# First attention's scores as three products of split operands, its rows one slot later, rotary steps behind them, and a last scaling out of SBUF in 640 and 384 columns

## The chip, the core and the metric

One core of one Trainium2 chip runs the whole program in one launch. The metric is device time in microseconds (us), the median of several runs. The engines are PE (TensorE, with its weight loads listed apart as PEld), DVE (VectorE), ACT (ScalarE), POOL (GpSimd) and SP (SyncE, which here mostly issues DMAs). Each engine works through its own row of instructions in order and waits on semaphores for what the others produce.

## The reference

A decoder trunk of two layers on 256 tokens of 1024 channels. Each layer norms its input, projects it, runs three token mixers side by side (the first attention, MLA, with 8 heads of 64 + 32 query and key columns; MoBA; retention), gates and sums them, and adds an MLP of squared ReLU. A last norm ends it. What the change touches:

```
def mla_branch(cq, ckv, k_rope, q_norm_g, kv_norm_g, w_q_up, w_kv_up, cos, sin):
    q = (rms_norm(cq, q_norm_g) @ w_q_up)            # per head: 64 "nope" + 32 rotary columns
    q = concat([q[..., :64], apply_rope(q[..., 64:], cos, sin)])
    kv = (rms_norm(ckv, kv_norm_g) @ w_kv_up)        # per head: 64 key + 64 value columns
    k = concat([kv[..., :64], broadcast(apply_rope(k_rope, cos, sin))])
    o = causal_attention(q, k, kv[..., 64:], 96 ** -0.5)
...
return rms_norm(x, final_norm)                       # after the last layer
```

## The kernel before

**Split products.** Nearly all products run on operands split in two rounded parts: a value is copied by ACT to fp32r (`hi`), and DVE subtracts to get `lo`. A product is then the three products hi·hi, hi·lo and lo·hi, added in PSUM (`three`, L297 to L300). Weights are split the same way when they arrive from HBM: `raw` (DMA on SP), `whi` (ACT, L277), `wlo` (DVE, L279), with six buffers of each. A `whi` can be written when PE's last product on the buffer's former holder has ended.

**Stages.** The tokens are two row tiles of 128. The projections of a layer run one after another as units: the compressed columns and MoBA's mq and mk first, then mv, then the gates (gmla0, gmla1, gmoba0, gmoba1), retention's rqk, rv and rg, the last gate, the branches' outputs, the output projection and the MLP. A unit of projection has four slots (0 to 3), and a slot of a 512-column unit has 12 products of 512 columns, six for each row tile. In between mv's slots stand MLA's own three products: qrope (the query's rotary columns, in PSUM tile pqr), qnope (the query's other columns, two PSUM tiles nope), kvup (the keys, two more tiles nope, and the values pv). All have the turned compressed columns `cTh` and `cTl` as one operand.

**What sets the order.** The program is a list `prog` of units; other steps are hung on a slot by `at(slot(unit, j), step)`. `attention(...)` hangs its groups of four heads (scores, softmax, a bounce of the probabilities through HBM that turns them, values) on slots counted from `first`. A list scheduler then orders each engine's row from the dependences, so a step that is moved in the list also moves its neighbours on ACT and DVE.

**Buffers.** PSUM has eight banks: four of tag `acc` (`acc_tile`: the projections' accumulators, and qnope's two tiles) and four of tag `misc` (pqr, kvup's tiles, scores, values of attention). A new tile takes a bank when the last reader of its former holder is done. In SBUF the tag `t4` has eight buffers of 4 x 256 columns: the four parts of the layer's input `xs0` to `xs3`, `cTh`, `cTl`, and later the attentions' outputs in hi and lo (`omlah`, `omlal` and so on).

**MLA's operands before.** `Q` and `KK` are f32 tiles of 128 partitions x 8 heads x 256 tokens. The nope tiles are copied by ACT from PSUM (L949, L950: 64 partitions at a time). The rotary part of the query is copied from pqr to `qr`, a swapped copy `qkoth` is fetched by DMA, and `qr_rope` multiplies both by tables (L982) and adds them in four steps of 64 partitions on DVE, straight into `Q` (L985, L986). A score product (L1005) is one f32 matmul of 128 columns and one of 256 for each head.

**MoBA's steps.** `moba_rope` rotates the rows of mq and mk on DVE, turns them in blocks and writes them to HBM; `fetch_turned` reads them back turned (`mqT`, `mkT`, DMAs on SP); `order_queries` copies the queries into `qkT` on ACT. MoBA's scores are L551.

**The end.** The last norm (L1545 to L1567) squares each row tile's halves on ACT (`fsq`, with the row sums in `fst`), takes root (ACT) and reciprocal (DVE, `fr`), and scales: the first half was multiplied by the gain `gf` on DVE beforehand (L1560) and is scaled on ACT (L1566); the other goes from PSUM in one step on DVE (L1563). Each half has its own DMA to HBM, on SP and on ACT's queue.

Of the kernel before, what the change touches and what calls it, by code (L numbers as in the profile page):

```python
# [7 lines left out]
F32 = mybir.dt.float32  # L8
F32R = mybir.dt.float32r
BF16 = mybir.dt.bfloat16  # L10
AF = mybir.ActivationFunctionType
ALU = mybir.AluOpType
AX = mybir.AxisListType

P = 128
D = 1024
S = 256
# [16 lines left out]
MLA_H, MLA_QR, MLA_KVR, NOPE, ROPE, VD = 8, 256, 128, 64, 32, 64  # L34
QKD = NOPE + ROPE
# [9 lines left out]

C_QNOPE = [QKD * h + i for h in range(MLA_H) for i in range(NOPE)]
C_QROPE = [
    QKD * h + NOPE + 16 * half + i for p in range(0, MLA_H, 2) for half in range(2) for h in (p, p + 1) for i in range(16)
]

C_MQ, C_MK = range(416, 928), range(928, 1440)
# [98 lines left out]
def trunk(ctx: ExitStack, tc: tile.TileContext, gx, wts, consts, gfin, gn, xtok, out):  # L150


    nc = tc.nc
    _, where, _ = weight_plan()
# [3 lines left out]
    sb = ctx.enter_context(tc.tile_pool(name="sb", bufs=1))  # L158
# [10 lines left out]
    K = cp.tile([P, K_DEC], F32, name="K")  # L169
# [16 lines left out]
    def load_w(*key):  # L186

        ahead = 0 if key[:2] in ((0, "b0"), (0, "mq"), (0, "b0mq")) else AHEAD
        have(min(ahead + 1, len(loaded) + len(order)))
        return loaded.pop(key)  # L190
# [99 lines left out]

    def w2k(name):
        return sb.tile([P, 512], F32, name=name, tag="w2k", bufs=W2K)

    def t4(name):
        return sb.tile([P, 4, S], F32R, name=name, tag="t4", bufs=T4)

    def three(o, ah, al, bh, bl, start, stop, **more):  # L297
        nc.tensor.matmul(o, ah, bh, start=start, stop=False, **more)  # L298
        nc.tensor.matmul(o, ah, bl, start=False, stop=False, **more)  # L299
        nc.tensor.matmul(o, al, bh, start=False, stop=stop, **more)  # L300
# [4 lines left out]
    def halves(tile_):  # L305
        return tile_.rearrange("p (two s) -> p two s", two=2)
# [11 lines left out]
    def split_plain(src, hi, lo):  # L318
        return nc.scalar.activation(hi, src, AF.Copy), nc.vector.tensor_sub(lo, src, hi.bitcast(F32))  # L319
# [451 lines left out]
    def at(slot, step):  # L771
        steps.setdefault(slot, []).append(step)

    def slot(key, j):
        return [k for k, _ in prog].index((key, j))
# [9 lines left out]
    def layer(l, xn, before):  # L785

        c0 = []
        c, mla, mqkv, rqkv = {}, {}, {}, {}
# [101 lines left out]
        def moba_rope(key):  # L890
            rope_rows(mrows[key], K[:, K_ROT_MB:K_DEC], MB_D // 8, w2k("mrot"))
            bounces[key] = written_rows(mrows[key], key, blocks_tile(key))

        def fetch_turned(key):
            qkT[key] = read_turned(bounces[key], key + "T", "tsums" if key == "mq" else "exch")
# [21 lines left out]

        def c_turn():
            c["h"], c["l"] = t4("cTh"), t4("cTl")
            mla["Q"] = sb.tile([P, MLA_H, S], F32, name="Q", bufs=1)  # L920
            KK = mla["K"] = sb.tile([P, MLA_H, S], F32, name="KK", bufs=1)
            mla["v"] = [w2k("vml") for _ in range(NT)]
            pts = [misc_tile("pct") for _ in range(2)]
            for k in range(3):
                pt = pts[k // 2][:, (k % 2) * S : (k % 2) * S + S]
                for t in range(NT):
                    nc.tensor.transpose(pt[:, P * t : P * t + P], c0[t][0][:, P * k : P * k + P], ident)
            pkr = pts[1][:, S : 2 * S]
            for t in range(NT):
                nc.tensor.transpose(pkr[:, P * t : P * t + P], krx[t], ident)  # L930
            for k in range(3):
                pt = pts[k // 2][:, (k % 2) * S : (k % 2) * S + S]
                split(pt, c["h"][:, k, :], c["l"][:, k, :], gain(G_CQ + 3 * l + k))
            nc.scalar.copy(KK[0:64, 1::2, :], pkr[0:64, None, :].to_broadcast([64, 4, S]))
            nc.scalar.copy(KK[64:P, 0::2, :], pkr[64:P, None, :].to_broadcast([64, 4, S]))

        at(slot("mk", 1 if l else 2), c_turn)

        def nope(dst, w, ks, copy, bank):
            for b in range(2):  # L940
                acc = bank("nope")
                for i in range(2):
                    cs = slice(P * (2 * b + i), P * (2 * b + i) + P)
                    for j, k in enumerate(ks):
                        three(
                            acc[:, S * i : S * i + S], w[0][:, j, cs], w[1][:, j, cs], c["h"][:, k, :], c["l"][:, k, :],
                            j == 0, j == len(ks) - 1,
                        )
                copy(dst[0:64, 4 * b : 4 * b + 4 : 2, :], halves(acc)[0:64])  # L949
                copy(dst[64:P, 4 * b + 1 : 4 * b + 4 : 2, :], halves(acc)[64:P])  # L950

        def qrope():

# [11 lines left out]
            mla["qo"] = swapped(mla["qr"])  # L965

        def qnope():
            nope(mla["Q"], load_w(l, "qnope", 0), (0, 1), nc.scalar.copy, acc_tile)

        def kvup():  # L970
            wh, wl = load_w(l, "kvup", 0)
            nope(mla["K"], (wh[:, :, 0:512], wl[:, :, 0:512]), (2,), nc.scalar.copy, misc_tile)
            for t in range(NT):
                acc = misc_tile("pv")
                sl = slice(P * t, P * t + P)
                three(acc, c["h"][:, 2, sl], c["l"][:, 2, sl], wh[:, 0, 512:1024], wl[:, 0, 512:1024], True, True)
                nc.scalar.activation(mla["v"][t], acc, AF.Copy)

        def qr_rope():
            qr, qo = halves(mla["qr"]), halves(mla["qo"])  # L980
            for i, o in enumerate((qr, qo)):
                nc.vector.tensor_mul(o, o, TAB_MLA[:, S * i : S * i + S][:, None, :].to_broadcast([P, 2, S]))  # L982
            for b in range(2):
                rows = slice(64 * b, 64 * b + 64)
                nc.vector.tensor_add(mla["Q"][64:P, 2 * b :: 4, :], qr[rows], qo[rows])  # L985
                nc.vector.tensor_add(mla["Q"][0:64, 2 * b + 1 :: 4, :], qr[rows], qo[rows])  # L986

        project(l, "mv", xn, 512, moba_done("mv"))
        for i, unit in enumerate((qrope, qnope, kvup)):
# [3 lines left out]
        omlaT, omobaT, oretT = [], [], []  # L993
        th_mla = gates(l, "gmla", xn)
        for i, key in enumerate(("mq", "mk")):
            at(slot("mv", i), lambda key=key: moba_rope(key))
            at(slot("gmla0", 2 * i), lambda key=key: fetch_turned(key))
        first = slot("mv", 3)
        at(first, lambda: omlaT.extend((t4("omlah"), t4("omlal"))))

        def mla_scores(h0):
            banks = [misc_tile("ps_s") for _ in range(4)]
            for h, bank in enumerate(banks, h0):
                for o, qs, ks in ((slice(0, P), slice(0, P), slice(0, P)), (slice(P, 3 * P), slice(P, S), slice(0, S))):
                    nc.tensor.matmul(bank[:, o], mla["Q"][:, h, qs], mla["K"][:, h, ks], start=True, stop=True)  # L1005
            return banks

        mla_last = attention(
            omlaT, lambda: mla["v"], QKD, first, mla_scores, (), MLA_GAP, MLA_TURN, MLA_MOVED, ("probT", "KK"),
            (l, "rg", 1), range(0, 4) if l else range(4, 8),  # L1010
        )
# [16 lines left out]
        def order_queries(h0):  # L1028
            qkT["q", h0] = in_order(qkT["mq"], h0 // 2)

        for i in range(2):
            at(slot("gmla1", 1 + i), lambda i=i: order_queries(4 * i))
        first = slot("gmoba1", 1)
        at(first, lambda: omobaT.extend((t4("omobah"), t4("omobal"))))

# [429 lines left out]
        for kind, i in mlp_order(l)[: -ENDS[l]]:  # L1465
# [11 lines left out]
            else:  # L1477
                w = load_w(l, "down", i, 0)
                for q in quarters:
                    down(w, h2[i], *q, i)  # L1480
                if last and i == NF - 8:
                    gf = sb.tile([P, D], F32, name="gf", tag="t4", bufs=T4)
# [64 lines left out]
        for t in range(NT):  # L1547
            y = sb.tile([P, D], F32, name="y", tag="t4", bufs=T4)
            r = sb.tile([P, 1], F32, name="fr", tag="st", bufs=SMALL)
            s0, s1, s2 = (st[:, 3 * t + i : 3 * t + i + 1] for i in range(3))  # L1550
            for half in range(2):
                cs = slice(512 * half, 512 * half + 512)
                ends[2 * t + half]()
                acc = accs[2 * t + half]
                if t == 0:
                    x_add(t, half)
                square(acc, 3 * t + half)
                if half == 0:
                    nc.vector.tensor_scalar(s2, s0, EPS, None, op0=ALU.add)
                    nc.vector.tensor_mul(y[:, cs], acc, gf[:, cs])  # L1560
            nc.scalar.activation(s1, s1, AF.Sqrt, bias=s2)
            nc.vector.reciprocal(r, s1)
            nc.vector.scalar_tensor_tensor(y[:, cs], acc, r, gf[:, cs], op0=ALU.mult, op1=ALU.mult)  # L1563
            nc.sync.dma_start(out[:, t, cs], y[:, cs])
            cs = slice(0, 512)
            nc.scalar.activation(y[:, cs], y[:, cs], AF.Copy, scale=r)  # L1566
            nc.scalar.dma_start(out[:, t, cs], y[:, cs])  # L1567
        order_pe.close()
# [19 lines left out]
W2K = 17  # L1588
# [96 lines left out]
```

## Time and profile before

| | |
|---|---|
| median of 3 runs | 802.57 us (802.55 to 802.66) |
| profiled execution | 802.47 us, span 800.4 us, mean granted clock 0.998 |
| PE busy | 792.7 us, 99% of the span |
| DVE busy | 654.8 us, 82% |
| ACT busy | 493.4 us, 62% |
| HBM traffic | 242 GB/s over the span |

The span is the time from the first to the last instruction of the profiled execution. In the rows of the profile an instruction has its line, its operation, `out<-in` by the program's names, and its shape; in a timeline the first number is the start in us and the second the busy time in us (of one instruction or, with x16, of a stretch of sixteen). Matmuls are pipelined: the time that one takes from the next is the distance of their starts, not its own duration. In the list of waits a row reads: who waited, for whom, then the sum in us, how often, and the longest. A row of the chain is a step of the work that ended last.

### The profile page before, as it was taken

The numbers are of one execution on the slowest core, as the hardware profiler recorded it, in microseconds if no ns is written. First come the engines' busy times: TensorE is split into PE (matmuls) and PEld (weight loads), VectorE is DVE, ScalarE is ACT, GpSimd is POOL, SyncE is SP. The second block draws the span as 40 slices with busy tenths as digits, with TensorE's granted clock in tenths as the row PEclk, the third lists the DMA queues.
The fourth block names the chain that finished last, engine by engine and source line by source line (L and its number), as shares of the span: only waits on it lengthen the run. The fifth ranks groups of instructions, "written<-read, shape, count | busy, mean of one in ns | idle before, by whom it ended". The sixth has DMA issues, their size and how long they took to land.

```text
span 800.4 us, 11136 instructions
## 1 busy us (share of the span) xinstructions
PE 792.7 (99%) x3819; PEld 660.3 (82%) x3819; DVE 654.8 (82%) x1129; ACT 493.4 (62%) x750; POOL 29.0 (4%) x32
## 2 busy tenths in 40 slices
PE   9999999999999999999999999999999999999996
PEld 7888887888888888888888888888888888888885
DVE  6779678878888888887796986788698879999794
ACT  7786665544557666666477765654545666666562
POOL 0100000000030000000020000000001200000000
PEclk9999999999999999999999999999999999999999
DMA  9979967965667867777655889587665687688841
GB/s 340 371 243 288 314 207 222 320 216 151 249 218 242 276 221 230 266 266 236 234 165 194 275 290 305 185 281 245 230 234 174 193 271 278 225 299 298 265 162 53
DMA packets 70280, 194.74 MB, mean 243 GB/s; under 512 B 8016, under 2 KB 27856, under 8 KB 70224
## 3 DMA queue, kind: packets, MB, share of 16 engines
q1 hardware_dynamic: 69648, 193.17, 73.2%
q10 hardware_dynamic: 576, 0.87, 0.3%
q8 instruction: 30, 0.49, 0.2%
q14 instruction: 26, 0.21, 0.1%
HBM read 171.46 MB, written 22.02 MB: 242 GB/s over the span
## 4 chain that ended last, share of the span: by engine, by line
PE 99%; DVE 0%; issue 0%; ACT 0%
PE acc L298 19%; PE acc L300 19%; PE acc L299 19%; PE pup L299 8%; PE pup L298 8%; PE pup L300 8%; PE acc L1240 6%; PE acc L859 1%; PE ps_s L1005 1%; PE po L645 1%; PE ps_s L551 1%; PE warm L765 0%; PE po L647 0%; PE ps_r L551 0%; PE b L865 0%; PE b L868 0%
## 5 line engine op out<-in xcount | busy, mean ns | idle before, releaser
L277 ACT ACTIVATE whi<-raw 128x1024 fp32r<-128x1024 f32 (+3 forms) x263 | 265.1, 1019 | 169.9 <-PE acc L300 102.3
L279 DVE TENSOR_TENSOR wlo<-raw,whi 128x1024 fp32r<-128x1024 f32 (+3 forms) x263 | 305.2, 1176 | 70.3 <-ACT whi L277 67.7
L298 PE MATMUL acc<-whi,xs 128*128 128x512 f32 (+1 forms) x384 | 150.2, 393 | 0.0
L299 PE MATMUL acc<-wlo,xs 128*128 128x512 f32 (+1 forms) x384 | 149.6, 390 | 0.0
L300 PE MATMUL acc<-whi,xs 128*128 128x512 f32 (+1 forms) x384 | 149.2, 390 | 0.0
L299 PE MATMUL pup<-wlo,xs 128*128 128x512 f32 x256 | 100.0, 391 | 0.0
L300 PE MATMUL pup<-whi,xs 128*128 128x512 f32 x256 | 99.8, 390 | 0.0
L298 PE MATMUL pup<-whi,xs 128*128 128x512 f32 x256 | 99.5, 390 | 0.0
L298 PEld LDWEIGHTS acc<-whi,xs 128*128 128x128 f32 x384 | 72.2, 188 | 15.7 <-ACT whi L277 0.7
L300 PEld LDWEIGHTS acc<-whi,xs 128*128 128x128 f32 x384 | 72.2, 188 | 14.2
L299 PEld LDWEIGHTS acc<-wlo,xs 128*128 128x128 f32 x384 | 72.2, 188 | 13.9
L300 PE MATMUL acc<-whi,sq 128*128 128x512 f32 x184 | 71.9, 391 | 0.0
L298 PE MATMUL acc<-whi,sq 128*128 128x512 f32 x184 | 71.9, 391 | 0.0
L299 PE MATMUL acc<-wlo,sq 128*128 128x512 f32 x184 | 71.7, 390 | 0.0
L300 PEld LDWEIGHTS pup<-whi,xs 128*128 128x128 f32 x256 | 48.1, 188 | 9.8
L299 PEld LDWEIGHTS pup<-wlo,xs 128*128 128x128 f32 x256 | 48.1, 188 | 9.7
L298 PEld LDWEIGHTS pup<-whi,xs 128*128 128x128 f32 x256 | 48.0, 188 | 9.8
L300 PEld LDWEIGHTS acc<-whi,sq 128*128 128x128 f32 x184 | 34.5, 188 | 7.7 <-DVE sq L319 0.6
L299 PEld LDWEIGHTS acc<-wlo,sq 128*128 128x128 f32 x184 | 34.6, 188 | 7.1
L298 PEld LDWEIGHTS acc<-whi,sq 128*128 128x128 f32 x184 | 34.6, 188 | 7.0
L573 ACT ACTIVATE prob<-prob,smx 128x128 f32<-128x128 f32 x64 | 28.3, 443 | 18.5 <-DVE smx L570 18.5
L1240 PE MATMUL acc<-mT,whi 128*128 128x512 f32 (+1 forms) x144 | 35.2, 371 | 0.0
(277 smaller groups left out, 1205.1 us busy)
## 6 DMA issues: line engine op xcount, KB each, us to landing
raw<-wts SPq DMA_DIRECT2D x264, 512.0 KB, 4.8
bounce<-hblocks SPq DMA_DIRECT2D x16, 512.0 KB, 3.7
hturned<-bounce SPq DMA_DIRECT2D x64, 128.0 KB, 3.1
pbounce<-blocks SPq DMA_DIRECT2D x8, 768.0 KB, 5.7
probT<-pbounce SPq DMA_DIRECT2D x32, 192.0 KB, 5.5
raw<-wts SPq DMA_DIRECT2D x5, 464.0 KB, 6.4
raw<-wts SPq DMA_DIRECT2D x4, 416.0 KB, 4.3
dec<-consts SPq DMA_DIRECT2D x2, 768.0 KB, 8.2
```

What stands on the lines that cost most here:

```text
L277: fetched.append(nc.scalar.activation(hi[:, cs], raw[:, cs], AF.Copy))
L279: nc.vector.tensor_sub(lo[:, cs], raw[:, cs], hi[:, cs].bitcast(F32))
L298: nc.tensor.matmul(o, ah, bh, start=start, stop=False, **more)
L299: nc.tensor.matmul(o, ah, bl, start=False, stop=False, **more)
L300: nc.tensor.matmul(o, al, bh, start=False, stop=stop, **more)
L551: mm = nc.tensor.matmul(bank[:, o], a[rows, sa], b[rows, sb_], start=True, stop=True)
L573: nc.scalar.activation(p[:, a:b], p[:, a:b], AF.Exp, bias=m[:, 2 + i : 3 + i], scale=d**-0.5, accum_out=m[:, 4 + i : 5 + i])
L645: nc.tensor.matmul(dst, vh, pT[h + j][0], start=True, stop=False)
L859: nc.tensor.matmul(mq[t][:, cs], a[:, P * t : P * t + P], wq[part][:, cs], start=first, stop=stop)
L1005: nc.tensor.matmul(bank[:, o], mla["Q"][:, h, qs], mla["K"][:, h, ks], start=True, stop=True)
L1240: nc.tensor.matmul(o, a, b, start=half == 0 and i == 0, stop=4 * half + n == KD and i == len(jobs) - 1)
```

## The change

**Scores.** `Q` and `KK` become fp32r tiles that hold the hi parts; their lo parts are `Ql` and `KKl`, each two tiles (four heads apiece) out of tag `t4`. The nope copies become a split: a hi copy on ACT and a lo subtraction on DVE for each 64 partitions. The key's rotary part is split once into `kr` and copied by ACT to `KK` and `KKl`. The query's rotary part is summed whole in `qr` (one DVE step), copied whole to `qrh` (ACT), and from there to `Q` in four ACT copies and to `Ql` in four DVE subtractions. Each score product becomes `three` on 128 and on 256 columns. The order of heads in `C_QROPE` changes with it, so that four heads that share a tile lie together.

**Places.** MLA's first group comes at gmla0 slot 0, not mv slot 3. MoBA's rotary steps come at gmla0 slots 2 and 3, not mv 0 and 1; their fetches at gmla1 1 and 2, not gmla0 0 and 2; the ordered queries at gmoba0 0 and 1, not gmla1 1 and 2.

**End.** Both halves of the last norm are multiplied by `gf` on DVE ahead of the reciprocal; then DVE scales 640 columns out of SBUF and ACT 384, with a DMA each of those widths.

```
+        def w2r(name):
+            return sb.tile([P, 512], F32R, name=name, tag="w2k", bufs=W2K)
...
         def c_turn():
-            mla["Q"] = sb.tile([P, MLA_H, S], F32, name="Q", bufs=1)
-            KK = mla["K"] = sb.tile([P, MLA_H, S], F32, name="KK", bufs=1)
+            for key in ("Q", "KK"):
+                mla[key] = sb.tile([P, MLA_H, S], F32R, name=key, bufs=1), [t4(key + "l") for _ in range(2)]
+            (KK, KKl), kr = mla["KK"], w2r("kr")
...
-            nc.scalar.copy(KK[0:64, 1::2, :], pkr[0:64, None, :].to_broadcast([64, 4, S]))
-            nc.scalar.copy(KK[64:P, 0::2, :], pkr[64:P, None, :].to_broadcast([64, 4, S]))
+            split_plain(pkr, kr[:, :S], kr[:, S:])
+            for rows, odd in ((slice(0, 64), 1), (slice(64, P), 0)):
+                nc.scalar.copy(KK[rows, odd::2, :], kr[rows, None, :S].to_broadcast([64, 4, S]))
+                for part in KKl:
+                    nc.scalar.copy(part[rows, odd::2, :], kr[rows, None, S:].to_broadcast([64, 2, S]))
...
-                copy(dst[0:64, 4 * b : 4 * b + 4 : 2, :], halves(acc)[0:64])
-                copy(dst[64:P, 4 * b + 1 : 4 * b + 4 : 2, :], halves(acc)[64:P])
+                for rows, odd in ((slice(0, 64), 0), (slice(64, P), 1)):
+                    split_plain(halves(acc)[rows], dst[0][rows, 4 * b + odd : 4 * b + 4 : 2, :], dst[1][b][rows, odd::2, :])
...
+            nc.vector.tensor_add(mla["qr"], mla["qr"], mla["qo"])
+            high = w2r("qrh")
+            nc.scalar.activation(high, mla["qr"], AF.Copy)
             for b in range(2):
                 rows = slice(64 * b, 64 * b + 64)
-                nc.vector.tensor_add(mla["Q"][64:P, 2 * b :: 4, :], qr[rows], qo[rows])
-                nc.vector.tensor_add(mla["Q"][0:64, 2 * b + 1 :: 4, :], qr[rows], qo[rows])
+                for to, odd in ((slice(64, P), 0), (slice(0, 64), 1)):
+                    nc.scalar.copy(mla["Q"][0][to, 4 * b + odd : 4 * b + 4 : 2, :], halves(high)[rows])
+                    nc.vector.tensor_sub(mla["Q"][1][b][to, odd::2, :], qr[rows], halves(high)[rows].bitcast(F32))
...
         for i, key in enumerate(("mq", "mk")):
-            at(slot("mv", i), lambda key=key: moba_rope(key))
-            at(slot("gmla0", 2 * i), lambda key=key: fetch_turned(key))
-        first = slot("mv", 3)
+            at(slot("gmla0", 2 + i), lambda key=key: moba_rope(key))
+            at(slot("gmla1", 1 + i), lambda key=key: fetch_turned(key))
+        first = slot("gmla0", 0)
...
                 for o, qs, ks in ((slice(0, P), slice(0, P), slice(0, P)), (slice(P, 3 * P), slice(P, S), slice(0, S))):
-                    nc.tensor.matmul(bank[:, o], mla["Q"][:, h, qs], mla["K"][:, h, ks], start=True, stop=True)
+                    three(bank[:, o], qh[:, qs], ql[:, qs], kh[:, ks], kl[:, ks], True, True)
...
-            at(slot("gmla1", 1 + i), lambda i=i: order_queries(4 * i))
+            at(slot("gmoba0", i), lambda i=i: order_queries(4 * i))
...
-                    nc.vector.tensor_mul(y[:, cs], acc, gf[:, cs])
+                nc.vector.tensor_mul(y[:, cs], acc, gf[:, cs])
             nc.scalar.activation(s1, s1, AF.Sqrt, bias=s2)
             nc.vector.reciprocal(r, s1)
-            nc.vector.scalar_tensor_tensor(y[:, cs], acc, r, gf[:, cs], op0=ALU.mult, op1=ALU.mult)
+            cs = slice(0, 640)
+            nc.vector.tensor_scalar(y[:, cs], y[:, cs], r, None, op0=ALU.mult)
             nc.sync.dma_start(out[:, t, cs], y[:, cs])
-            cs = slice(0, 512)
+            cs = slice(640, D)
             nc.scalar.activation(y[:, cs], y[:, cs], AF.Copy, scale=r)
```

The change also moves instructions that it does not name, since the scheduler orders the rows anew and the buffers go round differently. The rows below show where. Numbers behind names are of the build, and lines in rows of the changed kernel are its own (it has a few lines more: L837, L984 and L322 there are L834, L977 and the split copy).

**PE, layer 0, the end of mv and the start of gmla0.** Before, mv's last products write acc_498 and acc_499 and gmla0's first write acc_729, which has a bank that an early reader of nope had given back:

```order
L298 MATMUL acc_499<-whi_634,xs3_93 128x512
L299 MATMUL acc_499<-wlo_635,xs3_93 128x512
L300 MATMUL acc_499<-whi_634,xs3_93 128x512
L298 MATMUL acc_729<-whi_652,xs0_90 128x512
L299 MATMUL acc_729<-wlo_653,xs0_90 128x512
L300 MATMUL acc_729<-whi_652,xs0_90 128x512
```

Changed, mv writes acc_509 and acc_510, and gmla0's first tiles acc_678 and acc_679 have these two tiles' banks:

```order
L301 MATMUL acc_509<-whi_640,xs3_93 128x512
L302 MATMUL acc_509<-wlo_641,xs3_93 128x512
L303 MATMUL acc_509<-whi_640,xs3_93 128x512
L301 MATMUL acc_510<-whi_640,xs3_93 128x512
L302 MATMUL acc_510<-wlo_641,xs3_93 128x512
L303 MATMUL acc_510<-whi_640,xs3_93 128x512
L301 MATMUL acc_678<-whi_658,xs0_90 128x512
L302 MATMUL acc_678<-wlo_659,xs0_90 128x512
```

The order of PE's products is the same; the bank under the first of gmla0 is another.

**ACT, layer 0, around the copies of mv** (`mv<-acc` frees mv's banks; `vml<-pv` copies MLA's values). Before:

```order
L949 COPY KK_430<-nope_613 64x2x256
L950 COPY KK_430<-nope_613 64x2x256
L977 ACTIVATE vml_431<-pv_622 128x512
L977 ACTIVATE vml_432<-pv_627 128x512
L277 ACTIVATE whi_774<-raw_772 128x1024
L277 ACTIVATE whi_797<-raw_795 128x1024
L834 ACTIVATE mv_668<-acc_498,ms_293 128x512
L834 ACTIVATE mv_669<-acc_499,ms_293 128x512
```

Changed (whi_853 takes a buffer that mv's last product reads):

```order
L277 ACTIVATE whi_853<-raw_851 128x1024
L322 ACTIVATE Q_429<-nope_548 64x2x256
L992 ACTIVATE qrh_532<-qr_502 128x512
L984 ACTIVATE vml_436<-pv_628 128x512
L984 ACTIVATE vml_437<-pv_633 128x512
L837 ACTIVATE mv_674<-acc_509,ms_293 128x512
L837 ACTIVATE mv_675<-acc_510,ms_293 128x512
L996 COPY Q_429<-qrh_532 64x2x256 x4
```

A copy of the query, qrh and both value copies now stand between that whi and mv's copies.

**DVE, layer 0, ahead of qrh**, changed:

```order
L279 TENSOR_TENSOR wlo_774<-raw_771,whi_773 128x1024
L322 TENSOR_TENSOR KKl_433<-nope_606,KK_432 64x2x256
L322 TENSOR_TENSOR KKl_434<-nope_617,KK_432 64x2x256
L989 TENSOR_TENSOR qr_502<-qr_502,K_72 128x512
L989 TENSOR_TENSOR qkoth_504<-qkoth_504,K_72 128x512
L279 TENSOR_TENSOR wlo_792<-raw_789,whi_791 128x1024
L322 TENSOR_TENSOR Ql_430<-nope_548,Q_429 64x2x256
L322 TENSOR_TENSOR KKl_433<-nope_606,KK_432 64x2x256
L322 TENSOR_TENSOR KKl_434<-nope_617,KK_432 64x2x256
L990 TENSOR_TENSOR qr_502<-qr_502,qkoth_504 128x512
```

The five KKl and Ql rows are new, and the last row, which qrh reads, stands behind them.

**ACT, layer 1, around the same copies.** Before:

```order
L977 ACTIVATE vml_4166<-pv_4375 128x512
L977 ACTIVATE vml_4167<-pv_4380 128x512
L277 ACTIVATE whi_4527<-raw_4525 128x1024
L277 ACTIVATE whi_4550<-raw_4548 128x1024
L834 ACTIVATE mv_4421<-acc_4251,ms_4052 128x512
L834 ACTIVATE mv_4422<-acc_4252,ms_4052 128x512
```

Changed (whi_4602 waits for the product that fills pv_4444; gmla0's first two tiles have the banks of acc_4320 and acc_4321):

```order
L277 ACTIVATE whi_4602<-raw_4600 128x1024
L992 ACTIVATE qrh_4343<-qr_4313 128x512
L984 ACTIVATE vml_4229<-pv_4439 128x512
L984 ACTIVATE vml_4230<-pv_4444 128x512
L996 COPY Q_4222<-qrh_4343 64x2x256 x4
L277 ACTIVATE whi_4630<-raw_4628 128x1024
L322 ACTIVATE Q_4222<-nope_4359 64x2x256
L322 ACTIVATE KK_4225<-nope_4417 64x2x256
L322 ACTIVATE KK_4225<-nope_4428 64x2x256
L837 ACTIVATE mv_4485<-acc_4320,ms_4110 128x512
```

Seven copies of 64 partitions and qrh have come between the values and mv.

**DVE, the last row tile.** Before:

```order
L1559 TENSOR_SCALAR fst_7556<-fst_7556 128x1
L1560 TENSOR_TENSOR y_7597<-acc_6115,gf_7513 128x512
L1562 RECIPROCAL fr_7598<-fst_7556 128x1
L1563 SCALAR_TENSOR_TENSOR y_7597<-acc_6116,fr_7598,gf_7513 128x512
```

Changed:

```order
L1571 TENSOR_SCALAR fst_7672<-fst_7672 128x1
L1572 TENSOR_TENSOR y_7714<-acc_6231,gf_7629 128x512
L1572 TENSOR_TENSOR y_7714<-acc_6232,gf_7629 128x512
L1574 RECIPROCAL fr_7715<-fst_7672 128x1
L1576 TENSOR_SCALAR y_7714<-y_7714,fr_7715 128x640
```

The second product with the gain, which follows the last square, stands ahead of the reciprocal.

More of the change, by code (lines that the diff above doesn't have):

```diff
@@ L47 @@
 C_QROPE = [
-    QKD * h + NOPE + 16 * half + i for p in range(0, MLA_H, 2) for half in range(2) for h in (p, p + 1) for i in range(16)
+    QKD * h + NOPE + 16 * half + i for p in (0, 4, 2, 6) for half in range(2) for h in (p, p + 1) for i in range(16)
 ]
@@ L933, in c_turn, with nope @@
                 split(pt, c["h"][:, k, :], c["l"][:, k, :], gain(G_CQ + 3 * l + k))
-            nc.scalar.copy(KK[0:64, 1::2, :], pkr[0:64, None, :].to_broadcast([64, 4, S]))
-            nc.scalar.copy(KK[64:P, 0::2, :], pkr[64:P, None, :].to_broadcast([64, 4, S]))
+            split_plain(pkr, kr[:, :S], kr[:, S:])
[3 more added lines that the diff above has]
+                    nc.scalar.copy(part[rows, odd::2, :], kr[rows, None, S:].to_broadcast([64, 2, S]))
         at(slot("mk", 1 if l else 2), c_turn)
-        def nope(dst, w, ks, copy, bank):
+        def nope(dst, w, ks, bank):
             for b in range(2):
@@ L967, in qnope @@
         def qnope():
-            nope(mla["Q"], load_w(l, "qnope", 0), (0, 1), nc.scalar.copy, acc_tile)
+            nope(mla["Q"], load_w(l, "qnope", 0), (0, 1), acc_tile)
         def kvup():
             wh, wl = load_w(l, "kvup", 0)
-            nope(mla["K"], (wh[:, :, 0:512], wl[:, :, 0:512]), (2,), nc.scalar.copy, misc_tile)
+            nope(mla["KK"], (wh[:, :, 0:512], wl[:, :, 0:512]), (2,), misc_tile)
             for t in range(NT):
@@ L1003, in mla_scores @@
             for h, bank in enumerate(banks, h0):
+                (qh, ql), (kh, kl) = ((hi[:, h], lo[h0 // 4][:, h - h0]) for hi, lo in (mla["Q"], mla["KK"]))
                 for o, qs, ks in ((slice(0, P), slice(0, P), slice(0, P)), (slice(P, 3 * P), slice(P, S), slice(0, S))):
-                    nc.tensor.matmul(bank[:, o], mla["Q"][:, h, qs], mla["K"][:, h, ks], start=True, stop=True)
+                    three(bank[:, o], qh[:, qs], ql[:, qs], kh[:, ks], kl[:, ks], True, True)
             return banks
```

## The prediction

> **What bounds the kernel.** I read the page first (busy shares, then the chain that ended last), and the waits of PE and of all engines after it.
>
> ```profile
> PE 792.7 (99%) x3819; PEld 660.3 (82%) x3819; DVE 654.8 (82%) x1129; ACT 493.4 (62%) x750; POOL 29.0 (4%) x32
> ...
> PE 99%; DVE 0%; issue 0%; ACT 0%
> ...
> PE warm L765 <- PEq L1678: 0.8, 1, 0.8
> ...
> ACT whi L277 <- PE acc L300: 102.3, 76, 5.6
> ```
>
> The second row is the chain: TensorE is on it for 99% of the span. The third is the only wait of PE that the trace lists, 0.8 us at the very start. So all that PE gains or loses goes into the time one for one, and nothing can be gained elsewhere but in the tail behind the last product. ACT, in contrast, waits 102.3 us for PE's products to give weight buffers back: work added to ACT and DVE is free as long as PE finds its operands. Two questions remain: what the new score products cost PE, and whether PE must now wait for ACT somewhere.
>
> **The scores.** Before, a group of four heads is one stretch of PE:
>
> ```profile
> 60.76 2.62 PE ps_s L1005 x16
> ...
> 471.94 2.62 PE ps_s L1005 x16
> ```
>
> Two groups in each of two layers, 4 x 2.62 = 10.48 us. A group has 4 heads x (128 + 256) columns in two recorded passes, so 2.62 / (4 x 384 x 2) = 0.853 ns for a column of a pass. After, the four groups issue 48 products of 128 columns and 48 of 256, all on rounded fp32r halves. For these I need the spacing of starts, since the durations of pipelined products overlap:
>
> ```profile
> 45.18 0.28 PE L298 MATMUL pqr<-cTh,whi 128*128 128x256 f32 x1
> ...
> 48.78 0.40 PE L298 MATMUL pv<-whi,cTh 128*128 128x512 f32 x1
> ...
> 55.16 0.39 PE L300 MATMUL acc<-whi,xs 128*128 128x512 f32 x1
> ...
> 60.15 0.39 PE L298 MATMUL acc<-whi,xs 128*128 128x512 f32 x1
> ...
> 99.65 0.19 PEld L298 LDWEIGHTS acc<-whi,xs 128*128 128x128 f32 x1 [0.33 <-ACT whi L277]
> 99.76 0.19 PEld L299 LDWEIGHTS acc<-wlo,xs 128*128 128x128 f32 x1
> ```
>
> From 45.18 to 48.78 run 30 products of 256 columns, 0.120 us each; from 55.16 to 60.15 run 22 of 512 columns, 0.227 each. A product of 128 columns on fp32r stands nowhere in the trace. Lower end: 0.120 less half of (0.227 - 0.120) is 0.067, if only columns count. Upper end: 0.22, if it still takes two passes of 128 x 0.853 = 0.109. I take 0.12: each product has a weight load ahead of it, and the last two rows show two loads beginning 0.11 apart with the array otherwise idle, so a narrower product would wait for its load. 96 x 0.12 = 11.52, less 10.48: **+1.04 us** (ends: 48 x 0.067 + 48 x 0.12 = 8.98, or -1.5; 48 x 0.22 + 48 x 0.12 = 16.3, or +5.8).
>
> The Trainium skill speaks for a smaller price: its page "TensorE: Matmul & The Clock Gate", section "Back-to-back issue gap", gives a stream of load and product pairs about 81 ns each at 128 columns. By it the scores would be an estimated 48 x 0.081 + 48 x 0.12 = 9.65 us, -0.8 instead of +1.0. The 0.11 between this trace's loads speaks against it; no run here shows the pair itself.
>
> **The wait in layer 0.** This is the largest term. Before, the PSUM banks of gmla0's two accumulators had been given back by the query nope products long before. After, those are read late (the low half of Q takes the buffers of cT and can't be written before the pv products end), and gmla0 gets the two banks that mv, the products directly ahead, has just filled. So PE's first product of gmla0 waits for ACT's copy mv_674. ACT's order ahead of that copy begins with whi_853, which waits for its buffer until mv's last product ends, one place ahead of the waiting product. PE thus stands still for ACT's whole row: whi, a 64-row copy to Q, qrh, two vml copies, mv_674. The prices:
>
> ```profile
> L277 ACT ACTIVATE whi<-raw 128x1024 fp32r<-128x1024 f32 x240 | 251.4, 1057 | 161.1 <-PE acc L300 96.1 <-PE pup L300 29.9 <-issue 12.8
> ...
> L949 ACT COPY Q<-nope 64x512 f32<-64x512 f32 x4 | 2.3, 578 | 0.0
> ...
> L977 ACT ACTIVATE vml<-pv 128x512 f32<-128x512 f32 x4 | 2.2, 596 | 0.0
> ...
> L834 ACT ACTIVATE mv<-acc,ms 128x512 f32<-128x512 f32 x4 | 2.6, 690 | 1.0 <-PE acc L300 1.0
> ...
> L219 ACT ACTIVATE sumhi<-wsum 128x512 fp32r<-128x512 f32 x12 | 7.4, 616 | 0.0
> ```
>
> In the bar's left part the second number is the mean of one in ns. For qrh I take the row of L219, the same shape and types. 1.06 + 0.58 + 0.62 + 2 x 0.60 + 0.69 = 4.14. Neighbours overlap a little, and the semaphores cost a little:
>
> ```profile
> 53.43 1.09 ACT L977 ACTIVATE vml<-pv 128x512 f32<-128x512 f32 x2
> 54.40 2.01 ACT L277 ACTIVATE whi<-raw 128x1024 fp32r<-128x1024 f32 x2
> ...
> 794.26 0.29 ACT L1561 ACTIVATE fst<-fst 128x1 f32<-128x1 f32 x1
> 794.59 0.16 DVE L1562 RECIPROCAL fr<-fst 128x1 f32<-128x1 f32 x1 [1.14 <-ACT fst L1561]
> ```
>
> Two whi take 2.01, not 2.11, so 0.1 off at each of three borders between 128-row steps. A hop is 794.59 - 794.55 = 0.04, twice. And a product ends later than the next could start (0.39 - 0.227 = 0.16). 4.14 - 0.3 + 0.04 (borders of the 64-row copy) + 0.16 + 0.07 = **4.1 us, the floor**. It holds however early everything else is.
>
> On top of it, qrh must wait for DVE, which forms the rotary sum (L990 of the changed kernel) at the end of a long row of its own: two wlo, five 64-row subtractions, two products with the table, the sum.
>
> ```profile
> L279 DVE TENSOR_TENSOR wlo<-raw,whi 128x1024 fp32r<-128x1024 f32 x240 | 290.0, 1223 | 64.8 <-ACT whi L277 62.1 <-PE acc L859 1.9
> ...
> 52.72 0.65 DVE L982 TENSOR_TENSOR qr<-qr,K 128x512 f32<-128x512 f32 x1
> 53.29 0.68 DVE L982 TENSOR_TENSOR qkoth<-qkoth,K 128x512 f32<-128x512 f32 x1
> 53.89 1.30 DVE L328 STREAM_TRANSPOSE mkblocks<-mkrows 128x512 f32<-128x512 f32 x2
> 55.22 0.69 DVE L985 TENSOR_TENSOR Q<-qr,qkoth 64x512 f32<-64x512 f32 x1
> 55.94 0.69 DVE L986 TENSOR_TENSOR Q<-qr,qkoth 64x512 f32<-64x512 f32 x1
> ```
>
> 2 x 1.22 + 5 x 0.72 (55.22 to 55.94) + 2 x 0.585 (52.72 to 53.89) + 0.69 = 7.9 us, from the whi whose wlo begins the row. ACT covers the same stretch in six 64-row copies and three whi, 6 x 0.595 + 3 x 0.97 = 6.5. DVE is 1.4 later; I take 1.3 of it as wait, which makes **5.4 us** (4.1 if DVE is early; 6.5 if it comes to this row a wlo late).
>
> **The wait in layer 1.** The same pair of banks, with more between. ACT's whi_4602 waits for the last pv product; then follow qrh, two vml, four copies of qrh to Q, a whi, one 64-row copy to Q, two to KK, and mv_4485, for which gmla0's first product waits: 2 x 1.06 + 0.62 + 2 x 0.60 + 7 x 0.595 + 0.69 = 8.8, less 0.4 of overlap, plus 0.16 + 0.07, 8.6 us. PE meanwhile has 24 products of mv and 7 of the first scores: 24 x 0.227 + 7 x 0.12 = 6.3. Floor 2.3; half of layer 0's DVE delay on it, 0.6, gives **2.9 us** (1.5 if the score products are dearer, 4.5 if DVE's whole row is late).
>
> **The steps that move.** MoBA's rotary steps, their two turned fetches and the ordered queries come later, with the DMAs that they issue on SP. I cost them at nothing:
>
> ```profile
> 60.31 0.31 SPq L500 DMA_DIRECT2D mkT<-rowsbounce  x1
> ...
> 72.45 0.33 SPq L619 DMA_DIRECT2D pbounce<-blocks  x1
> ...
> L551 PE MATMUL ps_s<-mkT,qkT x64: 269/374/379, 98.1 to 521.0; 64*128 64x128 f32 x32, 64*128 64x256 f32 x32
> ```
>
> mkT was asked for until 60.31 and first used at 98.1, a cover of 38 us. Now its fetch stands on SP behind pbounce, the first MLA softmax's way out, which was issued at 72.45 and comes one slot (12 products, 2.7 us) and the wait (5.4) later, near 80.6. The first MoBA scores move to about 104 by the same waits and the dearer scores, so some 20 us of cover are left; without it those scores, and PE with them, would wait for mkT. The weight fetches that SP issues behind pbounce stood behind it before as well. MLA's first softmax has the gates as cover. The extra splits (8 copies on ACT and 8 subtractions on DVE in each layer, four of each for the rotary part, four copies for the low half of K) lie in ACT's 102.3 us of waiting, except where they stand in the two rows of ACT above.
>
> **The tail.** The last row tile ends:
>
> ```profile
> 792.76 0.68 DVE L1560 TENSOR_TENSOR y<-acc,gf 128x512 f32<-128x512 f32 x1
> ...
> 794.79 0.72 ACT L1566 ACTIVATE y<-y,fr 128x512 f32<-128x512 f32 x1 [0.23 <-DVE fr L1562]
> ...
> 794.79 0.75 DVE L1563 SCALAR_TENSOR_TENSOR y<-acc,fr,gf 128x512 f32<-128x512 f32 x1
> ...
> L582 DVE TENSOR_SCALAR prob<-prob,smx 128x256 f32<-128x256 f32 x20 | 7.0, 348 | 0.0
> L582 DVE TENSOR_SCALAR prob<-prob,smx 128x128 f32<-128x128 f32 x20 | 5.4, 269 | 0.3
> ```
>
> The scaling of 640 columns from SBUF is 0.35 + 3 x (0.348 - 0.269) = 0.585 against 0.75, -0.17; ACT's 384 columns save about 0.1. But the second product with gf now stands on DVE between the last square and the reciprocal, and waits for the same ACT step as the square root: it starts as the root starts (794.26) and lasts 0.68, so the reciprocal comes at 794.94 - 0.08 of overlap, not at 794.59: +0.28. Together **+0.15** with the larger first transfer (-0.1 to +0.5).
>
> **The sum.** 1.04 + 5.4 + 2.9 + 0.15 = 9.5. The profiled execution took 802.47 us (span 800.4), 0.1 under the median of 802.57. 802.5 + 9.5 = **812.0 us**, 1.2% slower. Two runs of this kernel can be told apart from about 0.2%, 1.6 us.
>
> **The rivals.**
>
> *Narrow products in two passes.* If a 128-column product costs 0.22, the scores cost +5.8 instead of +1.0, and layer 1's wait falls by a few tenths: some 816.6. For it: the f32 form of that width does it. Against: the operands are the fp32r halves that run in one pass at 256. 0.20.
>
> *The clock after a long wait.* The trace shows PE at half pace once, at its start after idleness:
>
> ```profile
> 0.77 4.00 PE warm L765 x9
> ```
>
> Nine products of 512 columns in 4.00 us are 0.44 each, against 0.227. If a wait of 5.4 us makes PE fall back to that and it takes the same 4 us to recover, half of those are lost, 2 us, up to 3.4 if the recovery is longer; layer 1's shorter wait does nothing. 814 to 815.5. No wait of PE over 0.8 us is in the trace, so nothing there speaks against it. 0.25. The Trainium skill has this as a rule (page "TensorE: Matmul & The Clock Gate", section on the HAM clock gate): half rate is the default, and an idle window of about 3.4 us brings it back. By that rule a wait of 5.4 us may or may not hold a whole window; the trace agrees for the start and can't show the fall.
>
> *Short waits.* If ACT's row runs nearer to the floors and the narrow products cost 0.08: -0.9 + 4.1 + 1.5 to 2.3, 807 to 809. 0.10.
>
> *Not slower.* The score products alone decide: at 0.067 they give -1.5, and at no wait the time would be 801.1. This holds only from where both waits together stay under 3 us, that is if gmla0's banks come free before mv's copy. The floor of 4.1 in layer 0 speaks against it, since ACT's order and its wait on mv's last product are fixed. 0.03.
>
> **The numbers.** Main case (809.5 to 814) 0.42, the four rivals 0.58. Range 807.5 to 819.0: it takes in the dear products and the clock, and leaves out the two of both at once and the cheapest end. Faster by over 0.2% 0.01, within 0.2% 0.02, slower 0.97.
>
> **What would show it.** PE's waits list one before gmla0's first product on ACT's mv, two times, near 5.4 and 2.9 us. The score groups take about 2.9 us each; 5 would be the two-pass case, 2.2 the cheap one. Matmuls at 0.43 spacing behind the wait would be the clock. The tail's reciprocal starts 0.3 later behind the last square. I am wrong if PE lists no such wait, or if MoBA's scores wait for mkT.

## The result and the profile after

The changed kernel takes 813.35 us (median of four runs, 812.29 to 814.56) against 802.57: ratio 1.0134, interval 1.0121 to 1.0146. Its profiled execution took 814.56 us, span 812.4, so the trace below has to explain 12.1 us.

The page of the changed kernel: busy shares, granted clock in 40 slices, and the chain that ended last. Then the waits of PE (who waited for whom, sum in us, how often, the longest).

```profile
PE 798.5 (98%) x3851; PEld 664.3 (82%) x3851; DVE 668.4 (82%) x1151; ACT 504.2 (62%) x770; POOL 29.1 (4%) x32
...
PEclk9998999999999999999999999999999999999999
...
PE 94%; ACT 4%; issue 1%; DVE 1%; DMA 0%
...
PE acc L301 <- ACT mv L837: 5.8, 2, 4.9
PE ps_s L301 <- ACT KK L322: 1.2, 1, 1.2
PE warm L768 <- PEq L1691: 0.8, 1, 0.8
```

Where the page of before had 99% of PE on the chain and no wait but the first, there are now two waits for mv's copy and one for a key's copy, and one slice of the clock below nine tenths. The place in layer 0, PE's row in time:

```profile
54.00 0.39 PE L302 MATMUL acc<-wlo,xs 128*128 128x512 f32 x1
54.23 0.39 PE L303 MATMUL acc<-whi,xs 128*128 128x512 f32 x1
59.53 0.79 PE L301 MATMUL acc<-whi,xs 128*128 128x512 f32 x1 [4.91 <-ACT mv L837]
60.12 0.63 PE L302 MATMUL acc<-wlo,xs 128*128 128x512 f32 x1
60.55 0.63 PE L303 MATMUL acc<-whi,xs 128*128 128x512 f32 x1
```

mv's last product starts at 54.23; the next should start 0.23 later and starts at 59.53: 5.07 us lost. Behind the wait the products start 0.43 apart, not 0.23. ACT's row over the same time:

```profile
54.65 1.06 ACT L277 ACTIVATE whi<-raw 128x1024 fp32r<-128x1024 f32 x1
55.73 0.59 ACT L322 ACTIVATE Q<-nope 64x512 fp32r<-64x512 f32 x1
57.16 0.63 ACT L992 ACTIVATE qrh<-qr 128x512 fp32r<-128x512 f32 x1 [0.83 <-DVE qr L990]
57.81 1.09 ACT L984 ACTIVATE vml<-pv 128x512 f32<-128x512 f32 x2
58.78 1.27 ACT L837 ACTIVATE mv<-acc,ms 128x512 f32<-128x512 f32 x2
```

It is the row of the order listing, step for step, with 0.83 us in it that ACT itself waits for DVE's rotary sum. In layer 1:

```profile
458.86 0.28 PE L303 MATMUL ps_s<-KK,Ql 128*128 128x256 f32 x1
460.39 0.33 PE L301 MATMUL ps_s<-KK,Q 128*128 128x128 f32 x1 [1.25 <-ACT KK L322]
461.59 0.79 PE L301 MATMUL acc<-whi,xs 128*128 128x512 f32 x1 [0.87 <-ACT mv L837]
462.18 0.63 PE L302 MATMUL acc<-wlo,xs 128*128 128x512 f32 x1
```

Without waits gmla0's first product would have started at 458.86 + 0.12 + 0.06 = 459.04; it started at 461.59, 2.55 lost in two pieces. And again the next products run slowly. The granted clock by stretches (the seventh value, behind POOL; the first is the stretch's length, the second PE's busy time):

```profile
55.00:58.80 3.80, 0.00 (x0) 0.00 (x0) 3.74 (x6) 2.92 (x6) 0.00 (x0) 1.00 0.49 146
58.80:65.60 6.80, 6.07 (x14) 4.79 (x15) 6.57 (x12) 4.31 (x8) 0.00 (x0) 0.50 0.46 154
65.60:70.00 4.40, 4.40 (x28) 3.87 (x27) 2.33 (x8) 1.06 (x1) 0.00 (x0) 0.99 0.29 119
...
458.20:461.60 3.40, 1.28 (x10) 0.89 (x8) 3.33 (x7) 3.35 (x6) 0.00 (x0) 1.00 0.57 167
461.60:465.00 3.40, 3.40 (x8) 2.72 (x9) 3.37 (x8) 2.05 (x3) 0.00 (x0) 0.50 0.27 96
465.00:470.00 5.00, 5.00 (x23) 4.11 (x23) 4.84 (x12) 1.35 (x5) 0.00 (x0) 1.00 0.40 144
```

The clock is at half for 6.8 us from 58.8, and for 3.4 us from 461.6. PE works in 6.07 and 3.40 of these, and half of that is lost: 3.0 and 1.7 us. The score products, a head and the start of the next:

```profile
68.19 0.22 PE L301 MATMUL ps_s<-KK,Q 128*128 128x128 f32 x1
68.25 0.28 PE L302 MATMUL ps_s<-KKl,Q 128*128 128x128 f32 x1
68.36 0.27 PE L303 MATMUL ps_s<-KK,Ql 128*128 128x128 f32 x1
68.47 0.33 PE L301 MATMUL ps_s<-KK,Q 128*128 128x256 f32 x1
68.64 0.28 PE L302 MATMUL ps_s<-KKl,Q 128*128 128x256 f32 x1
68.76 0.28 PE L303 MATMUL ps_s<-KK,Ql 128*128 128x256 f32 x1
68.88 0.22 PE L301 MATMUL ps_s<-KK,Q 128*128 128x128 f32 x1
...
70.94 0.40 PE L301 MATMUL acc<-whi,xs 128*128 128x512 f32 x1
```

A head takes 0.69 us for six products, 0.115 each; a group from 68.19 to 70.94 2.75 us, 0.13 more than the 2.62 of before. (By starts alone a group of before takes 2.43, from 60.60 to 63.03, but the product behind it then takes 0.42 to the next start and not 0.23. From four products ahead of a group to six behind it are 4.67 us before and 4.81 after, 0.14 more.) And the end, the last two transfers of the changed kernel (size, us from issue to landing):

```profile
y<-y SPq DMA_DIRECT2D x1, 320.0 KB, 2.5
y<-y ACTq DMA_DIRECT2D x1, 192.0 KB, 2.7
```

From the start of PE's last product (805.90) to the end of the span are 6.53 us; before it was 7.24 (793.12 to 800.35).

The account of the profiled execution: waits 5.07 + 2.55, half clock 3.0 + 1.7, scores 4 x 0.13 = 0.5, end -0.7, and a start that ran 0.26 earlier (the first product `b` at 5.35, before 5.61). That is 11.9 of 12.1.

### The profile page after: what moved, and what is told of

Read it like the earlier page. It is cut to its first block, busy times and chain, and to the rows that moved or that the text cites. A ratio compares the mean times of both kernels' runs of the same rounds, so it can differ in the third digit from the quotient of the medians.

```text
span 812.4 us, 11226 instructions
## 1 busy us (share of the span) xinstructions
PE 798.5 (98%) x3851; PEld 664.3 (82%) x3851; DVE 668.4 (82%) x1151; ACT 504.2 (62%) x770; POOL 29.1 (4%) x32
## 4 chain that ended last, share of the span: by engine, by line
PE 94%; ACT 4%; issue 1%; DVE 1%; DMA 0%
PE acc L301 18%; PE acc L303 18%; PE acc L302 18%; PE pup L302 8%; PE pup L301 8%; PE pup L303 8%; PE acc L1252 6%; PE acc L862 1%; ACT whi L277 1%; PE po L648 1%; PE ps_s L554 1%; ACT KKl L942 0%; DMA raw<-wts 0%; PE warm L768 0%; PE po L650 0%
## 5 line engine op out<-in xcount | busy, mean ns | idle before, releaser
L301 PEld LDWEIGHTS acc<-whi,xs 128*128 128x128 f32 x384 | 73.2, 191 | 22.3 <-ACT mv L837 6.4
L303 PEld LDWEIGHTS acc<-whi,xs 128*128 128x128 f32 x384 | 73.2, 191 | 14.8
```

## The experiments

My theory after the result: the low halves of the query take the buffers of `cTh` and `cTl`, so the nope banks come free late, so gmla0 gets mv's banks and waits for ACT, and the wait drops the clock. Rivals: the moved places make operands late; the extra splits alone do it. Each comparison below has a kernel before of its own on the same chip, whose medians were 802.58 to 802.80.

**One buffer more.** The changed kernel with

```
-T4 = 8
+T4 = 9
```

> The changed kernel with nine buffers of tag t4 in place of eight and nothing else. Theory: the low half of the query can't be written before the pv products give cT's buffers back; with a ninth buffer the order of buffers shifts, the query's nope banks are read and freed early as before the change, and gmla0 doesn't wait for mv's copies. PE then lists no wait but the 0.8 us at its start, the clock stays full, and what is left is the scores (four groups of 2.75 for 2.62 us, +0.5) and the tail (-0.8): 802.0 to 802.6 us. Rival: the extra splits on ACT and DVE, or the later steps, make the operands late whatever the banks: waits of some us stay, 808 to 813.

803.17 us (802.35 to 804.19), ratio 1.0004 (0.9995 to 1.0013). Its waits of PE:

```profile
PE warm L768 <- PEq L1691: 0.8, 1, 0.8
PE acc L303 <- DVE sq L322: 0.2, 1, 0.2
```

Both waits for mv's copies are gone, with all of the split's work still there, so the rival that this work is too much falls. ACT is no earlier than in the change (mv's copies start at 59.38 us, there at 58.78), and no product waits for them. Two of the four subtractions that form the low part of the query's nope columns now come early, at 49.29 and 52.50, before the second pv product starts at 52.76. The time is 0.6 above the upper end that I gave: the median lies 1.2 above that of the tail alone (below), and the scores explain 0.5 of it. A wait of 0.2 in the MLP is listed, and the end of its profile is 0.2 longer than in that of the tail alone (6.53 for 6.34 us); the rest I can't place.

**Other banks.** The changed kernel with eight buffers, and the query's nope tiles out of the other tag:

```
-            nope(mla["Q"], load_w(l, "qnope", 0), (0, 1), acc_tile)
+            nope(mla["Q"], load_w(l, "qnope", 0), (0, 1), misc_tile)
```

> The changed kernel with the query's nope tiles out of the tag misc in both layers, eight buffers of t4 as in the change. Theory: the low half of the query is as late as in the change, but gmla0's accumulators no longer have mv's banks, so the waits for mv's copies go, and with them the falls of the clock: 802.5 to 803.5, like the kernel with the ninth buffer. Rival, that the late low half costs PE its wait at the scores instead: 804 to 808.

803.36 us (802.68 to 803.87), ratio 1.0006 (0.9998 to 1.0015); of the waits for mv's copy 0.2 us is left. The other tag moves more than the bank, since the scheduler orders PE's row anew: in layer 0 MLA's second pv product starts at 64.00 us, in the change at 52.19, and the score products stand scattered among the gates'. The low half of the query comes later still (first at 66.34, in the change at 54.39), and PE lists no wait for it. So a late operand is not what PE waited for in the change. What this kernel and the one with nine buffers have in common is that gmla0 finds other banks, and both lose the waits.

**The places.** The kernel before with the diff's hunk on slots (moba_rope, fetch_turned, first, order_queries) and nothing else.

> The kernel before with the moved steps alone: MLA's first group at gmla0 0, MoBA's rotary steps, fetches and ordered queries later; scores one f32 product each, tail as before. Prediction's term: nothing, 802.5 to 802.7, and no wait of PE but the first. Rival: the later fetches or MLA's later softmax make the attention's products late; then a wait of PE on mkT, qkT or probT, over 803.5.

802.04 us (801.37 to 803.09), ratio 0.9991 (0.9982 to 1.0000). No wait of PE but the first, so the places cost nothing. That they seemed to gain 0.7 I had not expected; it is taken up below.

**The split at the old places.** The changed kernel with that hunk and the tail undone.

> The split scores alone, with MLA's first group and MoBA's steps at their old places and the tail as before. Theory: the wait comes of the buffers that the split takes, not of the places: PE waits 4.5 to 5.5 us for mv's copy in layer 0 and about 2.5 in layer 1, the clock falls as in the changed kernel, 812 to 815 us. Rival, that the moved places cause the waits: under 806.

812.71 us (812.35 to 814.09), ratio 1.0128 (1.0115 to 1.0142), the whole loss within the runs' spread. Its waits of PE, then three stretches of 3.41 us in layer 1, set where the clock could have changed (the last section says why there):

```profile
PE acc L301 <- ACT mv L837: 5.8, 2, 4.9
PE warm L768 <- PEq L1690: 0.8, 1, 0.8
PE ps_s L301 <- ACT KK L322: 0.7, 1, 0.7
PE ps_s L303 <- DVE Ql L997: 0.4, 1, 0.4
...
455.84:459.26 3.42, 2.75 (x15) 2.09 (x13) 3.34 (x6) 3.35 (x6) 0.00 (x0) 1.00 0.50 163
459.26:462.67 3.41, 2.18 (x9) 1.72 (x10) 3.38 (x6) 3.36 (x6) 0.00 (x0) 1.00 0.31 129
462.67:466.08 3.41, 3.41 (x17) 2.80 (x16) 3.30 (x11) 0.24 (x1) 0.00 (x0) 1.00 0.44 154
```

The wait in layer 0 is the same without the moves, and layer 1 has 2.0 us of waits: the rival that the places cause them falls. And in this execution layer 1's waits, 0.7, 0.4 and 0.9 us, left the clock at full.

**One wait at a time.** The changed kernel with `acc_tile` only in layer 1, or only in layer 0:

```
+            nope(mla["Q"], load_w(l, "qnope", 0), (0, 1), acc_tile if l else misc_tile)   # layer 1's wait alone
+            nope(mla["Q"], load_w(l, "qnope", 0), (0, 1), misc_tile if l else acc_tile)   # layer 0's wait alone
```

> The changed kernel, but in layer 0 the query's nope tiles come out of the tag misc instead of acc, so that gmla0 finds free banks; layer 1 as in the change. Theory: no wait in layer 0; layer 1's waits of 2.5 us stay, and 1.7 more if the clock falls there for one stretch of 3.4 us as it did in the profile: 804.5 to 805 without the fall, 806 to 807 with it. If a wait in two pieces of 1.25 and 0.87 us is too short for the clock to fall by itself and fell only as an echo of layer 0: 804.5 to 805 in all runs. Rival: layer 0 waits anyway, over 810.

807.62 us (806.53 to 808.09), ratio 1.0059 (1.0047 to 1.0072). PE's row behind the wait:

```profile
454.72 0.49 PE L301 MATMUL acc<-whi,xs 128*128 128x512 f32 x1 [0.88 <-ACT mv L837]
455.05 0.39 PE L302 MATMUL acc<-wlo,xs 128*128 128x512 f32 x1
455.28 0.46 PE L303 MATMUL acc<-whi,xs 128*128 128x512 f32 x1
455.54 0.63 PE L301 MATMUL acc<-whi,xs 128*128 128x512 f32 x1
455.96 0.63 PE L302 MATMUL acc<-wlo,xs 128*128 128x512 f32 x1
```

The clock falls here with only 0.24 us of wait in layer 0, and 0.8 us after the products have resumed (the first three 0.33, 0.23 and 0.26 apart, then 0.42). So it is no echo, and it answers to the time just past, not to the moment. The time is that of the case with the fall, 0.6 above its upper end.

> The same the other way round: layer 0 as in the change, layer 1's nope tiles from misc. Theory: layer 0's wait of 5.1 us and the half clock behind it, 6.1 us long, 3.05 lost: 802.5 + 0.5 + 5.1 + 3.0 = 811; if the half clock lasts one stretch of 3.4 us only, 809.5; without it 808. No wait in layer 1.

809.79 us (809.33 to 810.11), ratio 1.0088 (1.0074 to 1.0101). Behind the first 0.8 us only the wait for mv is listed, 4.9 us. The stretches of 3.41 us around it:

```profile
54.02:57.43 3.41, 1.49 (x7) 0.91 (x5) 3.35 (x6) 3.01 (x4) 0.00 (x0) 1.00 0.85 293
57.43:60.85 3.42, 0.42 (x2) 0.38 (x3) 3.39 (x4) 2.77 (x5) 0.00 (x0) 1.00 0.42 120
60.85:64.26 3.41, 3.41 (x10) 2.64 (x9) 3.29 (x6) 2.57 (x5) 0.00 (x0) 0.50 0.76 268
```

The clock is at half in the last of these alone: one stretch, where the profile of the changed kernel had two. That is the case of 809.5.

**The tail, and the places once more.** The kernel before with the last scaling alone; then with 512 columns on each engine in place of 640 and 384:

```
-            cs = slice(0, 640)
+            cs = slice(512, D)
             nc.vector.tensor_scalar(y[:, cs], y[:, cs], r, None, op0=ALU.mult)
...
-            cs = slice(640, D)
+            cs = slice(0, 512)
             nc.scalar.activation(y[:, cs], y[:, cs], AF.Copy, scale=r)
```

> The kernel before with the change's last scaling alone (both halves times the gain ahead of the reciprocal, 640 and 384 columns scaled out of SBUF). Theory from the trace of the changed kernel, whose end is 6.53 us behind the last product's start where it was 7.24: 801.8 us, -0.7 to -0.8, by transfers that land 2.5 to 2.75 us after their issue where they took 3.5 to 3.7, although they are issued 0.1 later. Rival, my prediction's term: +0.15, so 802.7; then the shorter landing is chance of one execution.

802.01 us (801.46 to 802.42), ratio 0.9990 (0.9981 to 0.9999): the 0.7 that the trace showed.

> As the tail alone, but 512 columns on DVE and 512 on ACT, so the transfers are of 256 KB each as before; the scaling still reads SBUF and the second product with the gain still stands ahead of the reciprocal. If the sizes of the transfers made the gain: 802.8 to 803.0 (issued 0.2 to 0.3 later, landing as before). If the gain comes of the time or order at which the two are issued, or of the source: 801.8 to 802.2.

802.36 us (801.72 to 802.86), ratio 0.9994 (0.9985 to 1.0002), between the two expectations. Of its two transfers of 256 KB the one on ACT's queue was issued 0.1 later than that of the tail alone and took 2.85 us, the one on SP was issued 0.06 earlier and took 2.32; so the sizes are not what made the landing short. But the places alone, with the old scaling, had gained as much. Hence two runs on what they share:

> The kernel before once more, for one thing: how long its last two transfers take to land. In its first profile they took 3.5 and 3.7 us; in the kernel with the moved steps alone, whose last norm is the same code, they took 2.6 and 2.9. If the 3.7 belongs to this program, it shows again, and the tail's gain in the changed kernel is no work of the new scaling; if it was chance of one execution, they land in 2.6 to 2.9 here and the span from PE's last product to the end is 6.4, not 7.24.

The last two transfers of the kernel before, in this second profile, and below the line of dots those of the kernel with the places alone:

```profile
y<-y ACTq DMA_DIRECT2D x1, 256.0 KB, 3.7
y<-y SPq DMA_DIRECT2D x1, 256.0 KB, 3.5
...
y<-y ACTq DMA_DIRECT2D x1, 256.0 KB, 2.9
y<-y SPq DMA_DIRECT2D x1, 256.0 KB, 2.6
```

Same code, same sizes, issued at the same distance from PE's last product (2.42 and 2.45 us), and 0.8 to 0.9 apart in landing; the slow landing came back in the same program (803.32 us in its one run, and again 7.25 us from the start of PE's last product to the end). So it goes with the program before, and not with the code of its last norm. The other traces, one for each program, fit: the split at the old places, with the old last norm, has 3.2 and 2.7 us, and all seven kernels with 640 and 384 columns have 2.5 and 2.7 to 2.8.

> The kernel before with the moved steps and the last scaling, scores as one f32 product each: the change without its split. If the 0.7 us that the tail alone and the places alone each gained are two gains of their own, 801.2; if both gained the same thing, that the program's last transfers land in 2.6 to 2.9 us where those of the kernel before take 3.5 to 3.7, then 801.9 to 802.1, no better than either alone.

801.94 us (801.24 to 802.50), ratio 0.9988 (0.9979 to 0.9997): no better than either alone. There is one gain, not two, and any of the three programs gets it. This kernel, the change without its split, also has the lowest median of all, 0.1% under the kernel before, the interval's end at 0.03%; from the tail alone (802.01) and the places alone (802.04) it can't be told apart. What in a program decides how long those transfers take stays open.

## Why the prediction was right, and where it wasn't

The forecast of 812.0 lies 1.4 us under the median. Its mechanism, two waits for mv's copy, was right; that the number came so near is in part luck. In the profiled execution the half clock, which I had put at nothing, cost 4.7 us, and against it stand 0.3 and 0.4 that I had too much for the waits, 0.5 for the scores and 0.85 for the end.

| term | forecast | measured |
|---|---|---|
| wait in layer 0 | 5.4 | 5.07 |
| wait in layer 1 | 2.9 | 2.55 |
| scores | +1.04 | +0.5 |
| moved steps | 0 | 0, no wait (places alone) |
| tail's own work | +0.15 | +0.14 (last issue 2.59 behind PE's last product, was 2.45) |
| last landing | not seen | -0.85 (the end as a whole -0.7) |
| half clock | 0, a rival at 0.25 | 3.0 and 1.7 in the profile; by the mean clocks less in two of the four runs |

*The waits.* The chain from buffers to banks to ACT's row held, in both layers, and the two kernels that cut it (one more buffer; another tag) lost all of it (with the other tag but for 0.2 us). The floor of 4.1 is close to what the trace gives without DVE's part: 5.07 - 0.83 = 4.24. DVE's lateness was sized 1.3 and measured 0.83: DVE's row ran from 49.48 to 57.12, 7.6 us for my 7.9, and ACT, free for qrh at 56.32, had taken 6.9 since 49.44 for my 6.5. In layer 1 the halves of my sum did not come as one wait: 1.25 us of it was paid earlier, at the second head's scores, for a copy of KK, which stands ahead of mv's copy in the same row of ACT. The sum holds, the place that I named holds for the smaller part. (In that row qrh stands ahead of the values' copies, as in my sum; the remark below its listing has it behind them.)

*The scores.* The two-pass rival (0.22) is dead: 128 columns start a second or third product 0.11 apart. My reason, that a product waits for its load, fits these 0.11, but no run separates the load from the product. And the two loads that I took it from did not begin "with the array otherwise idle": a product of 512 columns starts with the first of them, at 99.65 us. The distances are 0.06, 0.11, 0.11 for the narrow products, 0.17, 0.12, 0.12 for the wide: the first narrow one of a head takes less, the first wide one more. On average 0.094 and 0.137, together 0.115 where I took 0.12; the remaining half microsecond of my error is that 96 products at 0.115 are 11.0, not 11.5. The 81 ns that the Trainium skill gives (page "TensorE: Matmul & The Clock Gate", section "Back-to-back issue gap") are below the 0.094 us that this mix shows.

*The moved steps.* The fetch of mkT is asked for until 86.1 us and first used at 106.3, the cover of 20 us that I had worked out; no product waits for it.

*The clock.* This was the step that failed. I held it for a rival beside the main case; it came on top of it. And I wrote that the trace of before could not show a fall. It does, at its end: PE's last product ends at 793.51, and the clock of the stretches behind it was

```profile
793.50:796.60 3.10, 0.01 (x1) 0.00 (x0) 0.92 (x2) 1.70 (x4) 0.00 (x0) 1.00 0.34 132
796.60:800.40 3.80, 0.00 (x0) 0.00 (x0) 0.00 (x0) 0.00 (x0) 0.00 (x0) 0.51 0.32 122
```

full for 3.1 us and half after. From this row the wait of 5.4 us had to be given a fall, and the forecast would have been 814 to 815, the upper end of what the four runs show. (How soon the clock goes can't be read from one trace: in the twelve here it falls 2.1 to 5.2 us behind the end of PE's last product.) I also said that layer 1's shorter wait does nothing; with the layer-1 wait alone the clock fell too.

*The tail.* The term was right for the scaling itself. The end was 0.7 shorter for another reason, which no view of before alone could give: that the old program's last landing is slow.

## What to carry to other kernels

When a change lengthens a tile's life, look past the tile: see which buffer the next unit gets and who must finish with it, in the engine's own order, before the first product can start. Price a wait of PE with the half clock behind it, up to 1.7 us more for each stretch of 3.4 us: here the wait of 5 us brought it in each of the three traces that have it, and waits of about 2 us together in two of three. Look for the granted clock at the end of the trace, where PE always falls idle, to see that it goes. A gain of a few tenths in the last transfers is checked against a program that leaves the tail alone before the tail gets the credit.

## What the runs showed that I had not expected

The half clock comes in stretches of 3.41 us: two and one in the changed kernel, one with each wait alone. In the traces' record of the clock every stretch between two changes is a whole number of 3.413 us: in the kernel before 232 at full up to the fall at the end, in the changed kernel 16 at full, 2 at half, 116 at full, 1 at half, 101 at full. So the changes lie on a fixed grid. Counted along it, the stretches of the twelve traces divide cleanly. At full clock, a stretch with PE busy for 1.32 us or less was always followed by one at half (1.28 with layer 1's wait alone, 0.42 with layer 0's, 1.32 at the end of the change without its split), and one with 1.49 or more never was (1.49 with layer 0's wait alone, 2.75 and 2.18 in the split at the old places). From half the clock came back after a stretch with 3.19 us busy (layer 0 of the split at the old places), not after one with 2.71 (layer 0 of the changed kernel, hence its two stretches).

So whether waits of 2 to 2.5 us drop the clock depends on whether one stretch takes nearly all of them. In layer 1 it did in the changed kernel and with that wait alone; in the split at the old places the waits lie in two stretches, and the clock stayed full. A wait of 5.07 us can't be spread so: shared evenly between two stretches it leaves each an estimated (2 x 3.41 - 5.07) / 2 = 0.9 us. The rule in the Trainium skill (page "TensorE: Matmul & The Clock Gate", section on the HAM clock gate) speaks of an idle window of about 3.4 us and of a free-running one; the length agrees, the emptiness doesn't. The grid fits the spread of the runs too: those of the changed kernel lie at 812.3 and 812.5 with a mean clock of 0.996, and at 814.2 and 814.6 with 0.992. The profiled one has 0.992 and three stretches at half; the split at the old places has 0.996 in its profile and one. That the unprofiled runs had as many is not shown.

ACT's 64-partition copies of 512 columns differ by form. As ACTIVATE with rounding, two together take 1.08 us (KK out of PSUM, at 52.34 in the changed kernel); as plain COPY before the change they started 0.60 apart; as CAST from `qrh`, four took 2.53 us. The source and the types differ with the form, and no run separates them. The splits of the nope tiles were thus no dearer on ACT than the copies they replaced; with the new copies ACT's busy time as a whole rose from 493.4 to 504.2 us.
